# A hybrid decoder layer: sample products in two column halves, and weights, one weight block and the last stage's first chunk queued elsewhere

## The chip, the cores and the metric

The kernel runs on one core of a Trainium2 chip. The metric is the device time of one execution in microseconds (us). Engines are named as in the profile: PE is TensorE (PEld its weight loads), DVE VectorE, ACT ScalarE, POOL GpSimd, SP SyncE, which issues most DMAs. Each engine runs its instructions strictly in the order in which they are queued.

## The reference

One inference step of a one-layer hybrid decoder: eight heads of dilated sliding-window attention beside four heads of an mLSTM matrix memory, with one input and one output projection, for a prompt of 2048 tokens and for 32 sample tokens (8 sequences of 4) that have a cache and a state of their own.

```python
hn = rmsnorm(x, norm_g)
u = hn @ w_in                       # 1024 -> 11 parts
qa, ka, va, za, qb, kb, vb, ob, zb, ib, fb = jnp.split(u, offsets, axis=-1)
# attention: rope on qa, ka; three patterns (window, dilation) = (128,1), (512,4), (2048,16),
# each a partial softmax (m, den, acc); the partials are combined
# mLSTM: qb|kb through a causal convolution of width 4 and SiLU, then in chunks of 128 tokens:
dlog = b[..., :, None] - b[..., None, :] + ic[..., None, :] - m_t[..., :, None]
dmat = jnp.exp(jnp.where(causal, dlog, NEG_INF))
sqk = jnp.einsum('bhtd,bhsd->bhts', qc, kc) * dmat
num = inter[..., None] * jnp.einsum('bhtd,bhde->bhte', qc, C) + jnp.einsum('bhts,bhse->bhte', sqk, vc)
# C, n, m carried to the next chunk; both branches gated by silu(z), then y = x + [att|mlstm] @ w_out
```

## The kernel before

Matrix products run in fp16 with every value split in a high and a low half, so one product of fp32 quality is three matmuls (lines 165, 166 and 167: high·high, high·low, low·high). The program has three stages.

**Projections** (0 to 572 us of the profiled span). Sixteen tiles of 128 prompt tokens meet five blocks of 512 weight columns; `unit(i, j)` is tile i with block j, 24 matmuls of 128x512. Between the units stand: the sample tokens' own projection (`SA.project`, five groups into `ps_dp`, lines 244 and 245), the conversion of six further weight blocks for the mLSTM (`weight_block(j)`, started at the tiles in `BLOCKS`; each ends in `mlstm_part(j)`, which multiplies the sample tokens by that block in two halves, `ps_dm`, lines 316 and 317), and the sample tokens' attention over their caches: a loop over eight sequences (`SA.scores`, lines 359 to 372: a DMA spreads the queries into `d_qb`, POOL multiplies two blocks of keys by them, DVE reduces the three products), then `SA.softmax` (lines 374 to 402, with `ps_den` on PE) and `SA.values`.

**Attention of the prompt** (572 to 893 us). Four pairs of heads, two heads each. `loads(pr)` queues the keys, queries and values of a pair; `head(L, h)` makes scores (`ps_s`), exponentials, transposes (`ps_t`, `th` and `tl`) and products with the values (`ps_o`). Between its steps PE gets other work: the transposes of keys and queries (`ps_k`, `ps_q`), the recurrent state of the sample tokens (class `SampleMLSTM`: `loads`, `prepare`, and `state(b)` for each of eight sequences, whose `dT<-state_C` load POOL copies on line 903) and the first q and k projections of the next stage (`ps_qk`, lines 1161 to 1163, a generator named `early`). After head 0, `prepare` is queued right behind that head's last value product and last POOL step (`issue_after`), and then the SP queue gets three of the mLSTM weight blocks (`wb`, 2 MB each) and the first tokens (`early_x`, 1 MB).

**mLSTM and output** (893 to 1533 us). For each chunk c of 128 tokens: `gate_rows(c)` loads the decay rows `Mb` (POOL adds a mask to them on line 1355, ACT takes four exponentials on line 1359); the convolution turns `ps_qk` into `qk` (ACT, POOL and DVE, lines 1169 to 1190); `gated` makes `ps_st`, `ps_num` and the state; `project_out` multiplies by the output weights `wo`. `loads(c)` fetches the gate `z` and the attention result `A`, which waits until the last attention store to `att_scr` has landed.

The order of each engine's instructions is set when the program is built, by a scheduler that weighs the instructions as the code emits them; `issue_after(x)` forces what follows it behind x on x's engine. The sample products have 64 stationary columns (32 tokens, high and low), so their results take 64 of the 128 partitions of a bank. `sample_sum` adds the high-token and low-token halves: one ACT copy (line 252) and one DVE step (line 256), 32x512 each. The wait for pool tiles is by tag: `dhalf` has one buffer, the banks `proj` have four.

## Time and profile before

| | us |
|---|---|
| median of 3 runs | 1531.36 |
| lowest, highest run | 1527.40, 1534.86 |
| the profiled execution, its own time | 1534.84 |
| its span in the profile | 1533.0 |
| PE busy | 1399.0 (91% of the span) |
| DVE busy | 969.3 (63%) |
| ACT busy | 729.9 (48%) |
| POOL busy | 450.0 (29%) |

The profiled execution took 1.84 us beyond its span and is at the upper end of the three runs. Busy shares are means over three stages that are limited by different things, so the question at each place is what PE waits for there. The profile also gives the granted clock of TensorE, 0.971 on the mean: it is at half in several short stretches, most of which lie about a stall of PE.

### The profile page before, as it was taken

What the parts mean: (1) busy time and instruction counts of PE and PEld (TensorE: products, weight loads), DVE (VectorE), ACT (ScalarE), POOL (GpSimd) and SP (SyncE); (2) the same over time, 40 slices, a digit from 0 to 9 for tenths busy, and PEclk for the clock granted to TensorE, in tenths of its full rate; (3) what the DMA queues carried; (4) which work ended last, traced back from release to release, by engine and by line L of the source; (5) the groups of instructions that cost most, each with busy time, mean ns of one, the idle gap of its engine ahead of it and who ended that gap; (6) DMA issues with size and microseconds to landing.
All of it is one profiled execution on the core that took longest, in us unless ns stands there. A gap on an engine that the chain in (4) does not pass through costs nothing.

```text
span 1533.0 us, 28802 instructions
## 1 busy us (share of the span) xinstructions
PE 1399.0 (91%) x10679; PEld 864.2 (56%) x10679; DVE 969.3 (63%) x2946; ACT 729.9 (48%) x1673; POOL 450.0 (29%) x749
## 2 busy tenths in 40 slices
PE   4899999999989996999898995879999999999996
PEld 2445444444433345878688963556666666666653
DVE  5753765667633246889686813667766666667665
ACT  5365234344344226888677832443444444444433
POOL 1360333443301004645347951211111111111110
PEclk9999999999999998999999997989999999999999
DMA  8354479769779838995948775562555565554312
GB/s 293 123 167 165 139 266 313 271 228 305 281 217 353 286 122 265 350 270 179 239 170 241 264 249 187 188 181 87 176 194 180 165 186 159 173 172 104 77 49 76
DMA packets 153404, 310.95 MB, mean 203 GB/s; under 512 B 13534, under 2 KB 102783, under 8 KB 142687
## 3 DMA queue, kind: packets, MB, share of 16 engines
q1 hardware_dynamic: 149166, 230.10, 48.3%
q0 software_dynamic: 3952, 78.75, 13.9%
q8 instruction: 84, 1.38, 0.4%
q14 instruction: 58, 0.47, 0.1%
q10 hardware_dynamic: 144, 0.26, 0.0%
HBM read 231.80 MB, written 144.38 MB: 245 GB/s over the span
## 4 chain that ended last, share of the span: by engine, by line
PE 32%; DMA 23%; DVE 13%; issue 5%; ACT 4%; POOL 3%; SPq 1%; POOLq 0%; DVEq 0%; ACTq 0%
DMA qi<-g_scr 5%; DMA Mb<-g_scr 5%; PE ps_t L1039 3%; DVE cd L1181 2%; PE ps_out L167 2%; DMA v<-v_scr 2%; DMA kn<-k_scr 2%; PE ps_out L165 2%; PE ps_out L166 2%; PE ps_proj L165 2%; PE ps_proj L167 2%; PE ps_s L1017 2%; PE ps_proj L166 2%; DMA d_kv<-cache_win_v 2%; PE ps_s L1018 2%
## 5 line engine op out<-in xcount | busy, mean ns | idle before, releaser
L165 PE MATMUL ps_proj<-wa,x 128*128 128x512 f16 x640 | 244.9, 385 | 6.8 <-ACT wa L552 4.3
L166 PE MATMUL ps_proj<-wa,x 128*128 128x512 f16 x640 | 245.2, 384 | 2.4 <-POOL wa L111 2.0
L167 PE MATMUL ps_proj<-wa,x 128*128 128x512 f16 x640 | 244.8, 383 | 1.0 <-ACT x L226 1.0
L1026 DVE CUSTOM_DVE_ANT_0 sc<-ps_s,mask,ncqk 128x256 f32<-128x256 f32 (+1 forms) x384 | 142.8, 422 | 26.5 <-PE ps_s L1018 10.4
L1028 POOL TENSOR_SCALAR sc<-sc,o 128x256 f32<-128x256 f32 (+1 forms) x272 | 112.9, 426 | 85.3 <-DVE o L1026 76.7
L1043 DVE SCALAR_TENSOR_TENSOR tl<-ps_t,th 128x512 f16<-128x512 f32 (+1 forms) x152 | 102.6, 681 | 37.8 <-ACT th L1042 37.2
L165 PEld LDWEIGHTS <-x 128*128 128x128 f16 x768 | 73.5, 98 | 93.6 <-issue 22.3
L167 PEld LDWEIGHTS <-x 128*128 128x128 f16 x768 | 73.3, 98 | 85.2 <-issue 11.5
L1181 DVE SCALAR_TENSOR_TENSOR cd<-pre,cw,cd 128x256 f32<-128x256 f32 x168 | 85.9, 516 | 51.5 <-ACT cd L1175 49.6
L166 PEld LDWEIGHTS <-x 128*128 128x128 f16 x768 | 73.1, 98 | 74.4 <-issue 4.9
L367 POOL TENSOR_TENSOR d_kv<-d_kv,d_qb 128x2048 f32<-128x2048 f32 x16 | 72.3, 4538 | 128.3 <-DMA d_qb<-ds_scr 99.6
L1042 ACT ACTIVATE th<-ps_t 128x512 f16<-128x512 f32 (+1 forms) x152 | 90.0, 592 | 37.6 <-PE ps_t L1039 34.8
L167 PE MATMUL ps_out<-wo,yt 128*128 128x512 f16 x256 | 94.9, 379 | 7.8 <-DVE yt L1278 7.0
L1039 PE MATMUL ps_t<-c_id,pr 128*128 128x128 f32 x600 | 100.2, 288 | 1.3 <-DVE tl L1043 1.1
L165 PE MATMUL ps_out<-wo,yt 128*128 128x512 f16 x256 | 97.3, 380 | 2.3 <-ACT yt L1280 1.4
L166 PE MATMUL ps_out<-wo,yt 128*128 128x512 f16 x256 | 97.1, 379 | 0.0
L1355 POOL TENSOR_TENSOR Mb<-Mb,big 128x512 f32<-128x512 f32 x16 | 20.3, 1268 | 249.4 <-DMA Mb<-g_scr 234.5
L1055 PE MATMUL ps_o<-v,th 128*128 128x65 f16 x600 | 80.0, 195 | 14.4 <-ACT th L1042 11.7
L1161 PE MATMUL ps_qk<-cx,wb 128*128 128x256 f16 x256 | 71.0, 277 | 18.3 <-ACT pre L1171 16.5
L1359 ACT ACTIVATE Mb<-Mb,gcols 128x128 f32<-128x128 f32 x64 | 20.5, 390 | 130.5 <-POOL Mb L1355 130.5
L1354 POOL TENSOR_TENSOR qi<-qi,qk 128x128 f32<-128x128 f32 x60 | 29.3, 516 | 171.6 <-DMA qi<-g_scr 162.2
L1056 PE MATMUL ps_o<-v,th 128*128 128x64 f16 x600 | 79.2, 195 | 0.0
(459 smaller groups left out, 3775.1 us busy)
## 6 DMA issues: line engine op xcount, KB each, us to landing
s_win_k<-cache_win_k POOLq DMA_DIRECT2D x32, 1022.0 KB, 8.5
s_win_v<-cache_win_v POOLq DMA_DIRECT2D x32, 1022.0 KB, 7.7
wf<-w_in SPq DMA_DIRECT2D x18, 1024.0 KB
d_kv<-cache_win_k SPq DMA_DIRECT2D x16, 1024.0 KB
d_kv<-cache_win_v SPq DMA_DIRECT2D x16, 1024.0 KB
A<-att_scr SPq DMA_DIRECT2D x16, 792.0 KB
w_scr<-wst SPq DMA_DIRECT2D x12, 1024.0 KB
att_scr<-o SPq DMA_DIRECT2D x9, 1056.0 KB
```

Of the source, the lines that this page charges most:

```text
L165: nc.tensor.matmul(ps, lhsT=xh, rhs=hi[:, kt, cols], start=kt == 0, stop=False)
L166: nc.tensor.matmul(ps, lhsT=xh, rhs=lo[:, kt, cols], start=False, stop=False)
L167: yield nc.tensor.matmul(ps, lhsT=xl, rhs=hi[:, kt, cols], start=False, stop=kt == KT - 1)
L367: nc.gpsimd.tensor_tensor(t, t, qb, ALU.mult)
L1026: nc.vector.tensor_tensor_reduce(sc[:, x:x + n], sp[:, x:x + n], G.mask[:, MASK_END[u[0]] - n:MASK_END[u[0]]], G.ncqk, BIG, ALU.add, ALU.m ...
L1028: pooled = nc.gpsimd.tensor_scalar(sc[:, x:x + n], sc[:, x:x + n], -1.0, nm, ALU.mult, ALU.add)
L1039: nc.tensor.transpose(out=tp[:, c * P:(c + 1) * P], in_=pr[:, c * P:(c + 1) * P], identity=G.idf)
L1042: nc.scalar.activation(th[:, :w], tp[:, :w], AF.Copy, scale=PSC)
L1043: nc.vector.scalar_tensor_tensor(tl[:, :w], tp[:, :w], PSC, th[:, :w], ALU.mult, ALU.subtract)
L1055: nc.tensor.matmul(o, lhsT=th[:, cs], rhs=V[:, 0:65], start=first, stop=False)
L1056: nc.tensor.matmul(o[:, 0:64], lhsT=th[:, cs], rhs=V[:, 66:130], start=False, stop=False)
L1181: eng.scalar_tensor_tensor(d, pre[:, j:j + 256], cw[:, ct, j:j + 1], d, ALU.mult, ALU.add)
```

## The change

It has four parts.

1. `sample_matmuls` and `mlstm_part` no longer add the product with a weight block's high half and that with its low half into the same 64 partitions. A new `sample_pair` puts the first into partitions 0 to 63 and the second into 64 to 127 of the bank. As many matmuls are issued as before. The sum now takes four quarters: ACT copies 64x512 and DVE adds 64x512 (`sample_quarters`), then ACT moves 32x512 and DVE adds 32x512. The output's sample products (`ps_c`) get the same with a tile `dh3`. All in all, ACT and DVE get 12 instructions more each.
2. `BLOCKS` names tile 13 in place of 12 for the fifth weight block. The first half of a block's `ps_dm` stands behind `unit(i, 3)` instead of `unit(i, 2)`, and the second half behind unit 1 of the next tile (`pending`) instead of behind its own tile.
3. `SampleMLSTM.prepare` is put behind all that was queued by then on PE, ACT, DVE and POOL (a new `behind_all`), and the loads of `wb` and `early_x` move behind all SP loads of the second pair of heads.
4. In the last stage `gate_rows(0)` is queued first and the loads of `wo` last, and `gated` of chunk 0 is put behind all that was queued on PE, ACT and DVE.

```diff
--- before
+++ after
-BLOCKS = (5, 7, 9, 11, 12, 14)
+BLOCKS = (5, 7, 9, 11, 13, 14)
...
+@contextmanager
+def behind_all(G, *engines):
+    with ExitStack() as st:
+        for e in engines:
+            st.enter_context(G.tc.issue_after(next(i for i in reversed(G.nc.cur_bb.bb.instructions) if i.engine == e)))
+        yield
...
+def sample_pair(nc, ps, x, hi, lo, first, last):
+    nc.tensor.matmul(ps[0:2 * NS], lhsT=x, rhs=hi, start=first, stop=last)
+    nc.tensor.matmul(ps[2 * NS:], lhsT=x, rhs=lo, start=first, stop=last)
+
 def sample_matmuls(nc, ps, xd, hi, lo, cols):
     for kt in range(KT):
-        x = xd[:, kt].rearrange("p a t -> p (a t)")
-        nc.tensor.matmul(ps, lhsT=x, rhs=hi[:, kt, cols], start=kt == 0, stop=False)
-        nc.tensor.matmul(ps, lhsT=x, rhs=lo[:, kt, cols], start=False, stop=kt == KT - 1)
+        sample_pair(nc, ps, xd[:, kt].rearrange("p a t -> p (a t)"), hi[:, kt, cols], lo[:, kt, cols], kt == 0, kt == KT - 1)
+
+def sample_quarters(nc, t, ps, sc):
+    nc.scalar.activation(t, ps[2 * NS:], AF.Copy, scale=sc[2 * NS:] if sc is not None else 1.0)
+    nc.vector.scalar_tensor_tensor(t, ps[0:2 * NS], sc[0:2 * NS] if sc is not None else 1.0, t, ALU.mult, ALU.add)
 
 def sample_sum(G, pool, out, ps, sc, n, tag="dhalf"):
-    t = pool.tile([P, 512], F32, tag=tag, name="dhalf")[:NS]
-    nc.scalar.activation(t[:, :n], ps[NS:2 * NS, :n], AF.Copy, scale=sc[NS:2 * NS])
-    a, b = ps[0:NS, :n], t[:, :n]
+    t = pool.tile([P, 512], F32, tag=tag, name="dhalf")[:2 * NS, :n]
+    sample_quarters(nc, t, ps[:, :n], sc)
+    a, b = t[0:NS], t[NS:]
...
-    nc.vector.scalar_tensor_tensor(out, a, sc[0:NS], b, ALU.mult, ALU.add)
+    nc.scalar.activation(out, b, AF.Copy)
+    nc.vector.tensor_tensor(out, out, a, ALU.add)
...
             for j in range(5 if i < NT - LATE else 3):
                 pe = unit(i, j)
-                if block is not None and j in (0, 2):
+                if pending is not None and j == 1:
+                    behind(pe, pending)
+                    pending = None
+                if block is not None and j in (0, 3 if i < NT - LATE else 2):
                     behind(pe, block)
...
             gate_unit(i)
-            if block is not None:
-                behind(pe, block)
+            pending = block
...
             L = loads(pr)
+            if pr == 1:
+                with behind_all(G, ENG.SP):
+                    for j in range(3):
+                        nc.sync.dma_start(out=G.wb[j], in_=G.w_scr[j])
+                    nc.sync.dma_start(out=G.early_x.rearrange("p a k t -> p (a k t)"), in_=G.x_scr[0])
             for h in range(2):
...
-                last = head(L, h)
+                head(L, h)
                 if pr == h == 0:
-                    SM.prepare(last)
-                    for j in range(3):
-                        nc.sync.dma_start(out=G.wb[j], in_=G.w_scr[j])
-                    nc.sync.dma_start(out=G.early_x.rearrange("p a k t -> p (a k t)"), in_=G.x_scr[0])
+                    with behind_all(G, ENG.PE, ENG.Activation, ENG.DVE, ENG.Pool):
+                        SM.prepare()
...
+        L = Ctx()
+        gate_rows(0, L)
         xg = [G.early_x, x_load(1)]
         big = one.tile([P, P], F32, tag="big", name="big")
         nc.sync.dma_start(out=big, in_=I["c_causal"])
-        L = loads(0)
-        gate_rows(0, L)
+        loads(0, L)
+        residual(0, L)
         for j in range(2):
             nc.sync.dma_start(out=wo[j], in_=G.w_scr[4 + j])
-        residual(0, L)
...
-            y = gated(c, L, qk, tok, vs[c], ogs[c])
+            with ExitStack() as st:
+                if c == 0:
+                    st.enter_context(behind_all(G, ENG.PE, ENG.Activation, ENG.DVE))
+                y = gated(c, L, qk, tok, vs[c], ogs[c])
```

The tables of the scheduler follow from that. Three places show what the code doesn't tell.

**The SP queue at the first heads.** Before, `wb_5075` to `wb_5077` are the three weight blocks, `qn` and `kn` the queries and keys of the second pair, `v_6680` its first values.

```order
L850 DMA dT<-sg_scr 128x128
L851 DMA dT<-dm_u 32x4x128
L1085 DMA wb_5075<-w_scr 128x8192
L1085 DMA wb_5076<-w_scr 128x8192
L1085 DMA wb_5077<-w_scr 128x8192
L1086 DMA early_x<-x_scr 128x4096
L666 DMA qn<-q_scr 128x16x256
L666 DMA kn<-k_scr 128x6144
L891 DMA dT<-state_C 128x4x128 x2
L865 DMA s_convT<-dT 128x192
L949 DMA v_6680<-v_scr 128x4160
```

After, with `v_6698` the last values of the second pair, and `kn` the keys of the third:

```order
L1125 DMA att_scr<-o_5148 128x16x132
L978 DMA v_6698<-v_scr 8x16x260 x14
L1103 DMA wb_5095<-w_scr 128x8192
L917 DMA s_C<-dT 128x4x128
L1103 DMA wb_5096<-w_scr 128x8192
L1103 DMA wb_5097<-w_scr 128x8192
L1104 DMA early_x<-x_scr 128x4096
L691 DMA kn<-k_scr 128x6144
L937 DMA dm_num<-dT 4x516
L914 DMA dT<-state_C 128x4x128
L917 DMA s_C<-dT 128x4x128
L972 DMA v_8335<-v_scr 128x4160
```

The four large loads stood ahead of the second pair's queries and keys; now they stand ahead of the third pair's keys, and of a `state_C` load.

**The ACT queue at the first head.** `th` and `pr` are steps of the attention; `dT<-dT,scols` (line 879, 902 in the changed kernel) is a step of `prepare`, which waits for POOL's line 876 (899). Before, in the middle of the first head's steps (`o_5130` to `o_5128` are its results):

```order
L1003 ACTIVATE o_5130<-ps_o 128x7x65
L1003 ACTIVATE o_5130<-ps_o 128x2x65
L1042 ACTIVATE th<-ps_t 128x512
L1032 ACTIVATE pr<-sc 128x512
L879 ACTIVATE dT<-dT,scols 32x32 x4
L1042 ACTIVATE th<-ps_t 128x512
L1032 ACTIVATE pr<-sc 128x512
L1042 ACTIVATE th<-ps_t 128x512
```

After, behind the first head's last results and among those of the next:

```order
L1026 ACTIVATE o_5148<-ps_o 128x7x65
L1065 ACTIVATE th<-ps_t 128x512
L1055 ACTIVATE pr<-sc 128x512
L1026 ACTIVATE o_5148<-ps_o 128x2x65
L902 ACTIVATE dT<-dT,scols 32x32 x4
L1065 ACTIVATE th<-ps_t 128x512
L1055 ACTIVATE pr<-sc 128x512
L1065 ACTIVATE th<-ps_t 128x512
```

The step of `prepare` moved from the 254th row to the 308th of ACT, past the rest of head 0.

**ACT and POOL where the last stage begins.** `Mb` of chunk 0 comes first, `Mb` of chunk 1 second; `qk_11736` and `qk_11756` are the last of chunk 0's four convolved pieces. ACT before:

```order
L1185 ACTIVATE qk_11736<-cd 128x256
L1200 ACTIVATE cv<-ps_v,cinv 128x4x128
L1359 ACTIVATE Mb<-Mb,gcols 128x128 x4
L1209 ACTIVATE og<-ps_og,bhinv 128x512 x2
L1359 ACTIVATE Mb<-Mb,gcols 128x128 x4
L1171 ACTIVATE pre<-ps_qk,cinv 128x256
L1169 ACTIVATE tail<-pre 128x3
L1175 ACTIVATE cd<-pre,cw 128x256
L1171 ACTIVATE pre<-ps_qk,cinv 128x256
```

ACT after; the next `Mb` rows, those of chunk 1, stand 25 rows below the first, behind all of chunk 1's `pre` and `qk` rows:

```order
L1384 ACTIVATE Mb<-Mb,gcols 128x128 x4
L1225 ACTIVATE cv<-ps_v,cinv 128x4x128
L1194 ACTIVATE pre<-tail 128x3
L1210 ACTIVATE qk_11756<-cd 128x256
L1225 ACTIVATE cv<-ps_v,cinv 128x4x128
L1234 ACTIVATE og<-ps_og,bhinv 128x512 x2
L1196 ACTIVATE pre<-ps_qk,cinv 128x256
L1194 ACTIVATE tail<-pre 128x3
L1200 ACTIVATE cd<-pre,cw 128x256
```

POOL before (`s_win` are copies of the caches that need no engine's result):

```order
L1184 TENSOR_TENSOR cd<-cd,qk_11736 128x256
L1183 TENSOR_SCALAR qk_11736<-pre,cw 128x256
L1184 TENSOR_TENSOR cd<-cd,qk_11736 128x256
L1189 TENSOR_TENSOR qk_11736<-qk_11736,cd 128x256
L1190 TENSOR_TENSOR qk_11736<-qk_11736,cd 128x256
L1355 TENSOR_TENSOR Mb<-Mb,big 128x512
L264 DMA s_win_k<-cache_win_k 16x16352 x3
L1355 TENSOR_TENSOR Mb<-Mb,big 128x512
L264 DMA s_win_k<-cache_win_k 16x16352
L264 DMA s_win_v<-cache_win_v 16x16352 x2
L1354 TENSOR_TENSOR qi<-qi,qk_11449 128x128
```

POOL after, from chunk 1's `Mb` on:

```order
L1209 TENSOR_TENSOR cd<-cd,qk_11756 128x256
L1380 TENSOR_TENSOR Mb<-Mb,big 128x512
L288 DMA s_win_k<-cache_win_k 16x16352
L288 DMA s_win_v<-cache_win_v 16x16352 x2
L1208 TENSOR_SCALAR qk_11756<-pre,cw 128x256
L1379 TENSOR_TENSOR qi<-qi,qk_11469 128x128
L1379 TENSOR_TENSOR qi<-qi,qk_11510 128x128
L1379 TENSOR_TENSOR qi<-qi,qk_11551 128x128
L1379 TENSOR_TENSOR qi<-qi,qk_11592 128x128
L1209 TENSOR_TENSOR cd<-cd,qk_11756 128x256
L1214 TENSOR_TENSOR qk_11756<-qk_11756,cd 128x256
L1215 TENSOR_TENSOR qk_11756<-qk_11756,cd 128x256
```

On ACT, chunk 1's exponentials no longer stand ahead of the first `pre` of chunk 1. On POOL, chunk 1's `Mb` used to stand behind all of chunk 0's convolution, and now stands ahead of its last four rows. On PE, 48 of chunk 0's 192 `ps_qk` matmuls that stood among the attention's now stand behind it, ahead of `ps_v`.

## Rows read from the trace of the kernel before

**Rows 1.** The page: busy time of each engine, share of the span, instructions.

```profile
PE 1399.0 (91%) x10679; PEld 864.2 (56%) x10679; DVE 969.3 (63%) x2946; ACT 729.9 (48%) x1673; POOL 450.0 (29%) x749
```

**Rows 2.** Windows: stretch, its length, each engine busy (instructions), granted clock, DMA share, GB/s.

```profile
147.00:166.00 19.00, 19.00 (x122) 9.89 (x121) 9.17 (x28) 6.45 (x11) 1.63 (x3) 1.00 0.42 147
355.00:416.00 61.00, 59.51 (x339) 28.31 (x338) 41.24 (x61) 26.33 (x51) 22.71 (x15) 1.00 0.80 274
416.00:436.00 20.00, 15.28 (x75) 7.04 (x74) 8.61 (x23) 10.10 (x25) 2.84 (x6) 0.96 0.81 263
```

**Rows 3.** Tile ps_dp: count, durations in ns (min/median/max), first and last start, forms.

```profile
L244 PE MATMUL ps_dp<-wa,xd x40: 379/379/403, 147.4 to 165.1; 128*64 128x512 f16 x40
...
L252 ACT ACTIVATE dhalf<-ps_dp,wainv x5: 679/679/680, 151.9 to 165.7; 32x512 f32<-32x512 f32 x5
```

**Rows 4.** Groups of PE, 209 to 420 us: count | busy, mean | idle before, its releaser.

```profile
L317 PE MATMUL ps_dm<-wst,xd 128*64 128x512 f16 x32 | 13.8, 430 | 8.6 <-DVE wst L113 8.3
```

**Rows 5.** The same view, 442 to 549 us.

```profile
L418 PE MATMUL ps_dv<-d_kv,d_sc 128*32 128x512 f32 x192 | 24.9, 601 | 1.6 <-DMA d_kv<-cache_win_v 1.6
```

**Rows 6.** Line 367 of the cache loop: starts, its waits, who waited for it.

```profile
L367 POOL TENSOR_TENSOR d_kv<-d_kv,d_qb x16: 4499/4522/4799, 173.3 to 395.4; 128x2048 f32<-128x2048 f32 x16
...
  DMA d_qb<-ds_scr: 99.6, 6
...
  DVE d_sc L372: 45.6, 7
```

**Rows 7.** Chain that ended last, 404 to 437 us: start, length, what.

```profile
414.11 13.18 DMA w_scr<-wst
...
435.85 1.06 PE ps_den L391 x2
```

**Rows 8.** Waits, 590 to 640 us: engine, line, waited for: total, times, longest.

```profile
POOL dT L876 <- DMA dT<-sg_scr: 13.6, 1, 13.6
...
PE ps_o L1055 <- ACT th L1042: 11.7, 1, 11.7
...
PE ps_k L678 <- DMA qn<-q_scr: 2.2, 1, 2.2
```

**Rows 9.** Chain that ended last, 590 to 640 us.

```profile
604.74 32.65 DMA kn<-k_scr
```

**Rows 10.** Windows of the attention.

```profile
595.00:605.00 10.00, 0.29 (x2) 0.13 (x2) 0.41 (x1) 1.88 (x6) 2.00 (x6) 0.50 0.69 160
605.00:609.00 4.00, 3.67 (x37) 3.36 (x38) 3.99 (x15) 2.93 (x8) 1.62 (x4) 0.55 0.96 406
633.00:636.00 3.00, 3.00 (x21) 2.75 (x20) 1.92 (x5) 2.68 (x7) 0.30 (x1) 0.51 1.36 506
675.00:725.00 50.00, 48.51 (x642) 39.62 (x640) 44.26 (x172) 40.53 (x85) 25.89 (x66) 1.00 0.66 220
```

**Rows 11.** Waits, 640 to 893 us.

```profile
POOL dT L903 <- DMA dT<-state_C: 21.5, 4, 10.9
...
PE ps_dn L912 <- POOL dT L903: 7.1, 1, 7.1
```

**Rows 12.** Waits, 893 to 960 us.

```profile
PE ps_qk L1161 <- ACT pre L1171: 16.5, 1, 16.5
```

**Rows 13.** Chain that ended last, 893 to 960 us.

```profile
912.18 21.98 DMA Mb<-g_scr
934.24 1.26 POOL Mb L1355
...
945.70 0.22 PE ps_st L1360 x2
```

**Rows 14.** Windows of the last stage.

```profile
937.00:943.00 6.00, 5.78 (x28) 4.13 (x28) 3.77 (x7) 2.79 (x9) 2.05 (x4) 0.50 1.14 467
1032.00:1066.00 34.00, 34.00 (x232) 21.43 (x230) 24.12 (x80) 12.56 (x36) 5.02 (x6) 1.00 0.37 113
```

**Rows 15.** Tile ps_c, the output product of the samples.

```profile
L244 PE MATMUL ps_c<-wo,dyt x16: 379/379/403, 1066.8 to 1073.9; 128*64 128x512 f16 x16
```

More of the change, by code (lines that the diff above doesn't have):

```diff
@@ L47 @@
 MASK_END = (5 * P, 3 * P, P)
+ENG = mybir.EngineType
 class Ctx:
@@ L290, in project @@
         ps = self.pp.tile([P, 512], F32, tag="proj", name="ps_dp", bufs=4)
-        sample_matmuls(nc, ps[:2 * NS], G.xd, hi, lo, slice(0, 512))
+        sample_matmuls(nc, ps, G.xd, hi, lo, slice(0, 512))
         inv = G.wainv[:, j:j + 1]
@@ L309, in mlstm_part @@
         G, nc = self.G, self.G.nc
-        ps = self.pp.tile([P, 512], F32, tag="proj", name="ps_dm", bufs=4)[:2 * NS]
+        ps = self.pp.tile([P, 512], F32, tag="proj", name="ps_dm", bufs=4)
         def use(half, t):
@@ L314, in use @@
                 kt = half * KT // 2 + i
-                x = G.xd[:, kt].rearrange("p a t -> p (a t)")
-                nc.tensor.matmul(ps, lhsT=x, rhs=t[:, 0, i], start=kt == 0, stop=False)
-                nc.tensor.matmul(ps, lhsT=x, rhs=t[:, 1, i], start=False, stop=kt == KT - 1)
+                sample_pair(nc, ps, G.xd[:, kt].rearrange("p a t -> p (a t)"), t[:, 0, i], t[:, 1, i], kt == 0, kt == KT - 1)
             if half:
@@ L852, in loads, with prepare @@
         nc.gpsimd.memset(self.v[:, :, 128:129], 1.0)
-    def prepare(self, after):
+    def prepare(self):
         G, nc = self.G, self.G.nc
         pre, d, th, tmp, cv, qk, qi, bm, Dm = self.pre, self.d, self.th, self.tmp, self.cv, self.qk, self.qi, self.bm, self.Dm
-        with G.tc.issue_after(after[1].ins):
-            nc.gpsimd.tensor_copy(pre[:, :, :, 0:3], cv)
+        nc.gpsimd.tensor_copy(pre[:, :, :, 0:3], cv)
         ps = self.ps("ps_du")
-        with G.tc.issue_after(after[0].ins):
-            for ct in range(8):
-                nc.tensor.transpose(out=ps[:, ct * NS:(ct + 1) * NS], in_=self.u[:, ct * P:(ct + 1) * P], identity=G.idf[:NS, :NS])
+        for ct in range(8):
+            nc.tensor.transpose(out=ps[:, ct * NS:(ct + 1) * NS], in_=self.u[:, ct * P:(ct + 1) * P], identity=G.idf[:NS, :NS])
         nc.vector.tensor_copy(pre[:, :, :, 3:7], ps[:, 0:8 * NS].rearrange("p (c b t) -> p c b t", c=8, b=NB))
@@ L1056, in head @@
                         nc.tensor.matmul(o[:, 0:64], lhsT=th[:, cs], rhs=V[:, 66:130], start=False, stop=False)
-                        done = nc.tensor.matmul(o, lhsT=tl[:, cs], rhs=V[:, 0:65], start=False, stop=last)
+                        nc.tensor.matmul(o, lhsT=tl[:, cs], rhs=V[:, 0:65], start=False, stop=last)
                         c += 1
@@ L1235, in x_load, with loads @@
             return x16
-        def loads(c):
+        def loads(c, T=None):
             rows = slice(c * P, (c + 1) * P)
-            T = Ctx()
+            T = T or Ctx()
             T.z = pool.tile([P, 2, 512], F32, tag="z", name="z", bufs=2)
```

18 lines of the change are left out of this document (10 added, 8 removed).

## The prediction, made before the changed kernel had run

> **What bounds the kernel now.** I read the busy times first: PE is busy 1399.0 of 1533.0 us [rows 1], so what can be won is matmuls that take less time, or one of PE's waits. Next the windows, to see where PE is not full, and the waits there, to see who was last. In the projections PE is nearly full, 59.5 of 61 us in 355 to 416 [rows 2], apart from waits ahead of `ps_dm` [rows 4] and a thin stretch from 416 to 436. In the attention the first head has a hole: 0.29 us of PE in 595 to 605 [rows 10], for a DMA that POOL waits for, and PE behind it [rows 8]. Later PE is full there, 48.5 of 50 us, with DVE at 44.3 and ACT at 40.5 close behind [rows 10]. Where the last stage begins there is a second hole, 16.5 us [rows 12]. After that PE is full, 34.00 of 34 us [rows 14]. The sum is made against the profiled execution, 1534.84 us (span 1533.0 and 1.84 around it); that stands 3.5 us above the median of 1531.36.
>
> **Column halves, projections.** In `ps_dp` the first matmuls of the 40 pairs start from 147.4 to 165.1 us [rows 3], so a pair takes 0.454 us, one matmul 0.227, and all 18.2. Do the two halves run at once? `ps_dv`, which uses quarters of the columns, is the nearest row: 192 matmuls of 601 ns in only 24.9 us [rows 5], so four to five are under way at a time. I take it that halves overlap as well: 18.2 becomes 9.1; at the other end nothing is won. The 32 pairs of `ps_dm` [rows 4] take 14.5 us at the same pace, of which half, 7.3, can go, and so can the 8.6 us that PE idles ahead of them [rows 4], since a block's products now stand a unit or more later. Were PE alone the limit, the projections would win 9.1 + 7.3 + 8.6 = 25 us.
>
> PE is not alone. The cache loop needs nothing from it: 16 multiplications of 4.5 us start from 173.3 to 395.4 us, POOL waits 99.6 us for `d_qb`, and DVE waits 45.6 us for POOL [rows 6]. DVE, which empties PE's banks, is queued in the order of that loop, so PE can't run far ahead of it; at the end PE waits for the loop's softmax at `ps_den`, 435.85 [rows 7]. So I count what the loop's chain wins: about 2 us by an earlier start (the sample rows come out of `project` sooner, but their sum has grown, below), and from the softmax, which stood 13.2 us behind the store of block 12's halves [rows 7]. That block is now at tile 13, behind the softmax; I take 8 of the 13. PE then has 18 matmuls of 0.227, 4 us, more to do behind `ps_den`. Net: 2 + 8 − 4 = 6 us won; ends 0 and 25.
>
> **The longer sum.** Each group of sample products now takes ACT 64x512, DVE 64x512, ACT 32x512, DVE 32x512, where one copy of 32x512 took 0.679 us [rows 3]. If the number of partitions costs nothing (an assumption), a group takes some 1.4 us more, with one `dhalf` buffer: five groups in `project`, four in `mlstm_part`, one of gates, two of the output. With four banks PE isn't held by that, and in 147 to 166 us DVE is busy 9.17 and ACT 6.45 of 19 [rows 2], which hides it. If that cover is gone, five times 1.4, 7 us, go into the loop's start. I count nothing beyond the 2 us above; ends 0 and −7.
>
> A group's 16 matmuls take 3.6 us and would take 1.8, while each step of its sum stays near 0.7 [rows 3]. The Trainium skill, "TensorEngine Tiling (Array Packing)", Performance Considerations, warns that tiling speeds up TensorE but not the emptying of PSUM, which may become the bottleneck. By it the five groups would follow each other at the sum's pace, four times 0.679 or 2.7 us, 13.6 in place of 9.1, and the time would be 4 us longer than I say. Its Tile-to-Partition Mapping adds that column tiling disables Fast Weight Load; no run shows yet what that does to these loads.
>
> **First head.** POOL waited 13.6 us for `dT`, and PE 11.7 us in the end [rows 8]; the waiting steps of `prepare` now stand behind head 0. The DMA won't land later, since only what follows it on its queue moves, and head 0's rest fills the time. So the 11.7 us go, and with them half clock: the granted clock is 0.50 in 595 to 605 and 0.55 in 605 to 609 with PE busy 3.67 us [rows 10], some 2 us. The next stall, 2.2 us for `qn` [rows 8], had its load, and `kn`'s of 32.65 us [rows 9], behind 7 MB of weights; these loads now go ahead of the weights. It too left half clock, 0.51 in 633 to 636 with PE busy 3.00 [rows 10], 1.5 us. The place holds 17 us.
>
> What is late next: the weights now stand ahead of the third pair's `kn` and of a `state_C` load. 7.3 MB at 406 GB/s [rows 10] are 18 us of DMA, issued at some 655 to 675 us; in 675 to 725 the DMAs are free a third of the time, 17 us [rows 10]. The order has also moved the third pair's key transposes and the state's copies down, so the two about meet. `state_C` loads already cost POOL 21.5 us in four waits and PE 7.1 in one [rows 11]; I take 5 us for another such wait, ends 0 (it just fits) and 18 (the whole transfer is waited for). Net: 12 us won; ends −1 and 17.
>
> **Start of the last stage.** Chunk 1's `Mb` lands 21.98 us after its issue, POOL takes it at 934.24 [rows 13], ACT's exponentials stand ahead of `pre`, and PE gets its banks back after 16.5 us [rows 12], at clock 0.50 until 943 with 5.78 us busy [rows 14], 3 us more. In the new order `pre` doesn't wait for it, so that stall goes. What is late next is POOL: the same `Mb` now stands ahead of the last rows of chunk 0's convolution, which `ps_st` needs. Chunk 0's `Mb`, as large, no longer goes just ahead of it; I estimate that it lands a third of its 22 us sooner, at 927. POOL has then 1.26 us for the mask [rows 13] and eleven shorter rows of some 0.6: 8 us, so 935. PE has, from the end of the attention at 893, 96 matmuls of 512 columns at 0.227 us and 48 + 96 `ps_qk` of 256 at half of that, 38 us, and comes there at 931. A new wait of 4 us; chunk 0's last `ps_st`, at 945.70 before [rows 13], comes at some 935, 11 us sooner. The 48 `ps_qk` are 5.4 us that the attention no longer has to do; with DVE at 88% there [rows 10] I give back 3. Net: 14 us; ends 4 (the `Mb` lands when it did) and 19 (no new wait).
>
> **Output of the samples.** 16 pairs of `ps_c` from 1066.8 to 1073.9 us [rows 15] take 7.6, on a PE without gaps [rows 14]: half, 3.8, less some for the longer sum, 3; ends 0 and 3.8.
>
> **Sum.** 6 + 12 + 14 + 3 = 35: 1534.84 − 35 = 1499.8. By the median it would be 1496.4. I forecast 1498, between the two. The ends of all terms together are −4 and 65 us.
>
> **The rivals.**
> PE alone is the limit of the projections: 25 us in place of 6, 1479. For it: PE is 98% full [rows 2]. Against: it already waits for the loop's end.
> The column halves don't run at once: the projections still win some 4 us by the loop, the output nothing: 1503. For it: no row shows halves of fp16. Against: the quarters [rows 5].
> The change doesn't do what it says at the last stage: chunk 1's `Mb` lands as late as before, and the wait comes back ahead of `ps_st`; 14 becomes 4, 1508. For it: `A`, ahead of it, must still wait for the attention's last store. Against: `pre`, and DVE behind it, go on meanwhile.
> The late weights collide, the one that ends on the other side. The third pair's `kn` and a `state_C` load stand behind 7.3 MB, as the second pair's `kn` did for 32.65 us [rows 9]. If PE waits for the whole 18 us, runs at half clock for 3 more, and each of four later states waits 10.9 us, as the longest did [rows 11], the price is 65 us, against 40 won elsewhere and here: 1558. It decides from a price of 40 us on. Against: the states' copies moved down. A price near 20, more likely, gives 1513.
>
> **How the numbers follow.** Forecast 0.5 (1487 to 1508), PE alone 0.1, halves 0.13, moved wait 0.12, collision 0.15 (0.1 near 20 us, 0.05 beyond 40). The range 1482 to 1522 leaves out PE alone and the full collision. A measurement of this kernel tells about 0.5%, 7.7 us, from no change. Faster by more, below 1523.7: 0.85. Within: 0.09. Slower: 0.06.
>
> **What would show it.** Right: pairs of `ps_dp` and `ps_c` some 0.23 us apart; no wait ahead of `ps_dm`; `ps_den` some ten us sooner with PE waiting for it; PE full from 590 to 620; no wait of 16 us for `pre`, but one of some 4 ahead of chunk 0's `ps_st`. Wrong: pairs still 0.45 us apart; POOL waiting over 11 us for `state_C`, or PE for `kn`, at the third pair; projections shorter by over 15 us.

## The result, and the profile after

The change made the kernel slower: 1550.6 us (median of four runs, 1544.45 to 1554.0) against 1533.11 of the kernel before on the same chip. The ratio is 1.0112, with a 95% interval of 1.0079 to 1.0145, so some 17 us were lost where 35 were forecast as won. The profiled execution took 1549.89 us, its span 1548.1. PE does the work with 13 us less of busy time than in [rows 1], and idles more; the page of after:

```profile
PE 1385.7 (90%) x10679; PEld 857.7 (55%) x10679; DVE 972.5 (63%) x2958; ACT 739.2 (48%) x1685; POOL 449.0 (29%) x749
```

Three times cut the span into parts: the start of the first score (`ps_s`), of the last value product of the attention (`ps_o`), and of the last output product (`ps_out`).

| us | before | after | difference | forecast |
|---|---|---|---|---|
| start to first score | 572.7 | 561.5 | −11.2 | −6 |
| attention (first score to last `ps_o`) | 320.3 | 320.1 | −0.2 | −12 |
| last `ps_o` to last `ps_out` | 630.3 | 656.8 | +26.5 | −17 |

Each column is one profile. Seven kernels (after and, of the experiments below, e1, e3, e4, e6, e7 and e9) have the same order of instructions on PE, DVE, ACT and POOL up to the first score; in their profiles it starts at 554.6 to 570.7 us, 562 on the mean. So the −11.2 holds to some 8 us.

**The column halves run at once.** The tiles `ps_dp` and `ps_c` of after (count, durations in ns, first and last start, forms):

```profile
L255 PE MATMUL ps_dp<-wa,xd x40: 379/379/403, 147.3 to 156.6; 128*64 128x512 f16 x40
L256 PE MATMUL ps_dp<-wa,xd x40: 379/379/403, 147.4 to 156.8; 128*64 128x512 f16 x40
...
L255 PE MATMUL ps_c<-wo,dyt x16: 379/379/403, 1078.1 to 1082.0; 128*64 128x512 f16 x16
```

40 pairs take 9.5 us in place of 18.2 [rows 3], 16 pairs of `ps_c` 3.9 in place of 7.1 [rows 15]: a pair starts every 0.24 to 0.26 us, where one matmul started every 0.23 before. The weight loads of these matmuls take 110 ns before and after.

**Projections.** The waits of PE from 166 to 436 us in after (line, waited for: total, times, longest). Nothing waits ahead of `ps_dm` [rows 4] any more, but PE now waits for its banks:

```profile
PE ps_proj L177 <- DVE t L536: 11.2, 3, 4.8
PE ps_xt L237 <- DVE dhalf L268: 5.3, 1, 5.3
```

POOL's reduction for the softmax, one row of the tile `d_mx`, comes 14.1 us sooner; before, then after:

```profile
L382 POOL PARTITION_ALL_REDUCE d_mx<-d_mx x1: 1082/1082/1082, 417.9 to 417.9; - x1
```

```profile
L404 POOL PARTITION_ALL_REDUCE d_mx<-d_mx x1: 1085/1085/1085, 403.8 to 403.8; - x1
```

**First head.** The waits from 570 to 640 us, and pieces of the chain there (start, length, what):

```profile
PE ps_k L703 <- DMA qn<-q_scr: 15.0, 1, 15.0
...
POOL dT L877 <- DMA dT<-dm_u: 13.8, 1, 13.8
```

```profile
581.88 7.91 DMA v<-v_scr
589.81 0.64 SPq L876
590.56 0.32 SPq L691
590.91 6.20 DMA qn<-q_scr
597.16 1.03 PE ps_k L703 x8
```

The hole of [rows 8] is still there. PE now comes to the second pair's query transposes at 582 us, where before it came there at 629: 76 score matmuls stand ahead of them in its order, before 160. Their load is issued only at 590.91, since SP first queues the first pair's values one behind the other. POOL waits 13.8 us as before, now on line 877, a memset in `SampleMLSTM.loads`, which the change did not move. Before, the same memset (line 852) stood one row behind the row of `prepare` that POOL waited for, and its own load landed 0.8 us later; in the waits of [rows 8] it is

```profile
POOL dT L852 <- DMA dT<-dm_u: 0.4, 1, 0.4
```

It runs 30.7 us behind the first score before, 31.0 after. The first pair of heads, from its first score to the second pair's, takes 74.5 us in both; the second pair takes 77.8 us before and 83.7 after, the third and fourth are 3.5 and 2.6 us shorter.

**Third pair.** The waits from 690 to 780 us. PE waits for the keys queued behind the late weights, POOL for states, as long as before [rows 11]:

```profile
POOL dT L926 <- DMA dT<-state_C: 22.3, 4, 9.7
...
PE ps_k L703 <- DMA kn<-k_scr: 14.3, 2, 10.8
```

In 675 to 725 us PE is busy 38.96 of 50 us at a granted clock of 0.86 (columns as in [rows 10], where it was 48.51 at 1.00, though after is some 11 us further on in its work):

```profile
675.00:725.00 50.00, 38.96 (x521) 33.51 (x520) 33.92 (x140) 32.67 (x66) 19.69 (x52) 0.86 0.78 297
```

**Start of the last stage.** The waits from 881 to 990 us, and the chain there:

```profile
POOL Mb L1380 <- DMA Mb<-g_scr: 47.1, 2, 35.7
ACT Mb L1384 <- POOL Mb L1380: 26.9, 2, 17.4
...
PE ps_v L177 <- ACT cv L1225: 13.2, 1, 13.2
...
PE ps_qk L1186 <- ACT pre L1196: 5.2, 1, 5.2
...
PE ps_v L177 <- ACT pre L1196: 3.9, 1, 3.9
```

```profile
895.08 20.67 DMA Mb<-g_scr
915.82 1.27 POOL Mb L1380
...
917.41 0.97 ACT Mb L1384 x3
918.38 0.58 ACT cv L1225
919.01 0.58 PE ps_v L177
...
950.33 1.18 ACT Mb L1384 x4
951.53 0.70 DVE W L1389
```

The stall of [rows 12] has become three. The longest, 13.2 us, ends when ACT empties a bank (`cv`), and ACT had stood 17.4 us at the exponentials of an `Mb` that POOL could not mask before it landed. By the buffer numbers of the program this `Mb` is chunk 1's, and the trace agrees: POOL had masked one `Mb`, the first queued, at 893 us already. Chunk 0's exponentials come only at 950 us, and the step that uses them, `W`, right behind. Of the two groups of `Mb` rows that "The change" finds on ACT, 25 rows apart, the upper is thus chunk 1's and the lower chunk 0's. The first `ps_out` starts 108.1 us behind the last `ps_o`, before 83.6.

### The profile page after: what moved, and what is told of

Its sections match the earlier page's. It is cut to its first block, busy times and chain, and to the rows that moved or that the text cites. A ratio compares the mean times of both kernels' runs of the same rounds, so it can differ in the third digit from the quotient of the medians.

```text
span 1548.1 us, 28812 instructions
## 1 busy us (share of the span) xinstructions
PE 1385.7 (90%) x10679; PEld 857.7 (55%) x10679; DVE 972.5 (63%) x2958; ACT 739.2 (48%) x1685; POOL 449.0 (29%) x749
## 3 DMA queue, kind: packets, MB, share of 16 engines
q0 software_dynamic: 3952, 78.75, 13.8%
## 4 chain that ended last, share of the span: by engine, by line
PE 37%; DMA 26%; DVE 17%; issue 6%; POOL 6%; ACT 6%; SPq 2%; POOLq 0%; DVEq 0%; ACTq 0%
DMA Mb<-g_scr 5%; DMA qi<-g_scr 4%; PE ps_proj L179 3%; PE ps_proj L177 3%; PE ps_proj L178 3%; DMA d_qb<-ds_scr 3%; PE ps_t L1062 3%; DMA kn<-k_scr 3%; DMA v<-v_scr 2%; POOL d_kv L389 2%; PE ps_out L179 2%; DVE cd L1206 2%; PE ps_out L177 2%; PE ps_out L178 2%; PE ps_s L1040 1%
## 5 line engine op out<-in xcount | busy, mean ns | idle before, releaser
L177 PE MATMUL ps_proj<-wa,x 128*128 128x512 f16 x640 | 245.2, 385 | 17.8 <-DVE t L536 11.2
L177 PEld LDWEIGHTS <-x 128*128 128x128 f16 x768 | 73.5, 98 | 97.9 <-issue 13.8
L1186 PE MATMUL ps_qk<-early_x,wb 128*128 128x256 f16 x256 | 71.6, 280 | 10.5 <-ACT pre L1196 9.5
```

The source lines that it names most:

```text
L177: nc.tensor.matmul(ps, lhsT=xh, rhs=hi[:, kt, cols], start=kt == 0, stop=False)
```

## Experiments

Ratios are to the kernel before on the same chip, with 95% intervals. That kernel took 1539 to 1544 us on these chips, some 10 more than in the trace of before, so stages are compared among the experiments. "Rest" is from the last `ps_o` to the last `ps_out`, in us of one profile; "late" counts those of chunk 0's 192 `ps_qk` matmuls that stand behind the attention's last score in PE's order (before 24, after 72; of these, 48 of after also stand behind the attention's last value product, and none of before).

| | ratio | interval | attention | rest | late |
|---|---|---|---|---|---|
| e1 parts 1 and 2 | 0.9921 | 0.9896–0.9945 | 319.6 | 637.7 | 24 |
| e2 parts 1, 2, 4 | 0.9917 | 0.9890–0.9944 | 321.0 | 638.6 | 24 |
| e3 parts 1, 2, 3 | 1.0017 | 0.9987–1.0046 | 326.1 | 649.6 | 72 |
| e4 after, weights early | 0.9899 | 0.9837–0.9962 | 323.7 | 630.7 | 4 |
| e5 e4, memset early | 0.9936 | 0.9909–0.9963 | 332.9 | 631.1 | 4 |
| e6 after, weights behind keys | 1.0009 | 0.9985–1.0033 | 321.2 | 649.3 | 24 |
| e7 after, exponentials in order | 0.9970 | 0.9948–0.9992 | 317.7 | 638.2 | 72 |
| e8 e5, exponentials in order | 0.9923 | 0.9894–0.9951 | 328.9 | 625.0 | 4 |
| e9 after, keys held | 1.0116 | 1.0081–1.0151 | 322.3 | 666.4 | 72 |
| e10 e8, keys held | 0.9893 | 0.9866–0.9919 | 324.6 | 630.5 | 24 |
| e11 e10, weights behind keys | 0.9867 | 0.9812–0.9921 | 312.8 | 622.6 | 4 |
| e12 part 1 | 1.0000 | 0.9969–1.0030 | 324.7 | 635.9 | 24 |
| e13 part 2 | 1.0019 | 0.9998–1.0040 | 320.6 | 635.1 | 24 |
| e14 e11 without part 1 | 0.9957 | 0.9935–0.9979 | 322.2 | 621.4 | 4 |

### Which part loses: e1, e2, e3

e1 is the kernel before with parts 1 and 2; e2 adds part 4, e3 part 3. From after, e1 and e2 take out

```diff
-                if pr == 1:
-                    with behind_all(G, ENG.SP):
-                        ... wb and early_x
...
-                    with behind_all(G, ENG.PE, ENG.Activation, ENG.DVE, ENG.Pool):
-                        SM.prepare()
+                    SM.prepare(last)
+                    ... wb and early_x
```

and e1 and e3

```diff
-                if c == 0:
-                    st.enter_context(behind_all(G, ENG.PE, ENG.Activation, ENG.DVE))
```

with the order of the last stage's first loads.

> The kernel before with parts 1 and 2 alone (column halves, later weight block). In the trace of the changed kernel the first scores of the attention start 11.2 us sooner than before, and the samples' output product takes 3.4 us less. If these two parts are independent of the rest, as both theories hold, this kernel is 12 to 15 us faster than before: 1518 to 1521 us. If the gain of the projections came from the other parts, or is given back at the waits of the attention, within 3 us of before.

> Parts 1, 2 and 4, without 3 (prepare and the weight loads as before). Theory F (part 4 makes the loss: chunk 0's exponentials are forced behind chunk 1's, which wait for a DMA): the 26 us that the changed kernel loses where the last stage begins are lost here too, 1540 to 1547. Rival W (part 3's late weights make it: the first q and k projections and their convolution are pushed behind the attention): the start of the last stage is as before, with its 16 us wait for pre, and the kernel is as fast as parts 1 and 2 alone, 1517 to 1521.

> Parts 1, 2 and 3, without 4. Theory F: the last stage starts without the 13 us wait for the banks of ps_v, and the kernel is near 1520. Rival W: 48 q and k projections and the convolution on POOL still stand behind the attention, POOL and ACT still make PE wait 15 to 25 us there, and the kernel is at 1540 to 1550.

Parts 1 and 2 win 0.8%, 12 us. Part 4 on them wins and loses nothing (0.9917). Part 3 costs 0.96%, 15 us (0.9921 to 1.0017), and in the profiles the rest is 12 us longer, the attention 6.5. By e2 and e3 theory F fails and rival W, the weights' place, holds. The waits of PE from 881 to 966 us in e1, e2 and e3:

```profile
PE ps_qk L1186 <- ACT pre L1196: 16.4, 1, 16.4
```

```profile
PE ps_qk L1186 <- ACT pre L1196: 11.9, 1, 11.9
PE ps_yt L1301 <- ACT yh L1340: 7.0, 1, 7.0
```

```profile
PE ps_qk L1186 <- ACT og L1234: 13.7, 2, 12.3
PE ps_qk L1186 <- ACT pre L1196: 5.2, 1, 5.2
PE ps_v L177 <- ACT pre L1196: 2.4, 1, 2.4
```

In e1 the stall is that of [rows 12], to 0.1 us. In e2 it is 4.5 us shorter, and 7.0 come back 40 us later: `pre` still waits there for ACT, which stands 14.7 us at chunk 1's exponentials. In e3 more is lost, ahead of work that the attention used to hide: 72 of chunk 0's `ps_qk` matmuls, which need `wb` and `early_x`, now stand behind its last score, 24 in e1 and e2. At the third pair e3 also waits 9.7 us for `kn`, e1 and e2 not at all.

### The weights' place alone: e4 and e6

e4 is after with the weights at their old place, so part 3 is reduced to `prepare`; e6 is after with the weights behind the second pair's queries and keys, ahead of its values. The edit of e6:

```diff
                 pair_loads(G, pr)
+                if pr == 1:
+                    with behind_all(G, ENG.SP):
+                        for j in range(3):
+                            nc.sync.dma_start(out=G.wb[j], in_=G.w_scr[j])
+                        ... early_x
```

> Parts 1, 2, 4 and the half of 3 that puts prepare behind head 0; the weight loads stay right behind head 0. Theory F: 1530 to 1540, since the start of the last stage is lost as in the changed kernel. Rival W: 1503 to 1512: 12 to 15 us from parts 1 and 2, some 10 from the first head's wait of 11.7 us, and no loss behind.

> The changed kernel, with the three weight blocks and early_x queued on SP behind the second pair's keys and queries, but ahead of its values. In this order 24 of chunk 0's q and k projections are left behind the attention (72 in the changed kernel, 24 before), and the third pair's kn no longer stands behind the weights. Theory W (the place of the weight loads behind the values makes the loss): the 10.8 us wait for kn at 702 and the 9 us of waits for pre behind the attention go, the 15 us wait for qn stays: 0.985 to 0.995. Rival F (part 4 makes the loss): 1.000 or more.

With all else as in after, early weights give 0.9899 in place of 1.0112: 33 us for the order of four DMAs. e4 leaves 4 matmuls, after 72. e6 takes the wait for `kn` at the third pair away and leaves 24, but still measures 1.0009, where theory W had put it at 0.985 to 0.995, with 12.9 us for `qn` at the first head and 8.7, 5.8 and 7.0 at the start of the last stage. Its rest is 11 us longer than e2's, which also leaves 24 and has the same forced order. All of it falls ahead of the first `ps_out`, where PE idles 6.8 us longer than in e2 and is busy 4.0 longer with as many matmuls; where these waits come from no run separates. So the number of late matmuls is not all that the weights' place costs.

In e4 `prepare` stands behind head 0, and the first head still has its hole; waits from 580 to 645 us, and the load of the next pair's queries in the chain:

```profile
POOL dT L877 <- DMA dT<-dm_u: 13.5, 1, 13.5
...
PE ps_o L1078 <- ACT th L1065: 12.3, 1, 12.3
```

```profile
587.61 27.51 DMA qn<-q_scr
```

### The first head's wait: e5, e9, e10

e5 is e4 with the memset of one column ahead of the DMA that fills the others.

```diff
+        nc.gpsimd.memset(self.v[:, :, 128:129], 1.0)
         nc.sync.dma_start(out=self.v[:, :, 0:128], ...)
-        nc.gpsimd.memset(self.v[:, :, 128:129], 1.0)
```

> As e4 (parts 1, 2, 4, prepare behind head 0, weights early), but POOL's memset of the column beside a loaded tile, in SampleMLSTM.loads, is queued ahead of that tile's DMA instead of behind it. In e4 PE still waited 12.3 us at 590, and POOL 13.5 us in that memset for the DMA. Theory M (the memset is what holds the first head): the 12 us wait goes, and with it half clock: 10 to 14 us below e4, ratio 0.980 to 0.984 against before. Rival S (the serial loads of the values on SP hold the head's next products too): PE waits there for v or qn instead, at most 3 us gained, 0.988 to 0.990.

POOL's wait goes and head 0 ends earlier: the second head's scores begin at 592.6 us (598.4 in e4). Then PE waits for the next pair's queries, whose load now stands right behind the weights; waits from 580 to 645 us and chain:

```profile
PE ps_k L703 <- DMA qn<-q_scr: 16.1, 1, 16.1
```

```profile
596.89 27.92 DMA qn<-q_scr
```

The 12.3 us came back as 16.1, and the first pair takes 80.0 us (e4 72.3). This is a load that nobody had waited for long while PE was late. e9 and e10 hold the second pair's transposes further back, near where they stood before the change (behind 168 score matmuls; before 160, after 76), e9 in after, e10 in e8 (below):

```diff
+            if L.pr == 1 and h == 0:
+                with G.tc.issue_after(G.mark.ins):
+                    stacks(G, h, st, ...)
...
```

where `G.mark` is a score matmul of the 13th batch of the second head.

> The changed kernel with one edit: the transposes of pair 1's queries and keys for its first head are held behind the 13th score batch of head (0,1), so they stand at ps_s index 168 in TensorE's queue, where the changed kernel has them at 76. Nothing else is told to move. Theory 'only the place': the 15.0 us of idle TensorE at 597 us (ps_k behind the DMA of qn) were a wait for a load that lands near 612 us; at index 168 TensorE comes to it near 625 us, so the wait is gone, no other takes its place beyond the 10 us of the memset, and the first head ends some 5 to 12 us sooner; ratio to before 1.000 to 1.007 (the changed kernel 1.0112). Rival 'the wait is the load's chain': the memset still holds GpSimd near 590 us until dT lands, TensorE waits there in its place (10 us or more, as in the experiment on parts 1 and 2), and the time stays at 1.010 to 1.013. The late weights' other waits (kn at the third pair, the start of the last stage) stay in both.

> The kernel of e8 (parts 1 and 2, prepare behind head 0, weights at their old place, the memset ahead of its DMA, the last stage's first gate rows first, the exponentials of chunk 1 in the order of GpSimd) with pair 1's transposes held behind the 13th score batch of head (0,1). In e8 TensorE waited 15.9 us at 622 us for qn, whose load was queued right behind the 7.3 MB of weights. Theory 'the 7.3 MB must pass': qn lands near 638 us whatever stands ahead on TensorE; the transposes are due at index 168, near 620 us, so TensorE still waits 5 to 16 us: ratio to before 0.989 to 0.993, as e8 (0.9923). Rival 'only the place': the wait is gone and the ratio is 0.983 to 0.986.

e9 measures 1.0116, as after: the wait for `qn` is gone, and the memset's stands in its place. (The expectation has the load landing at 612 us; 597 is right, the wait ends there.) In e10 the 7.3 MB must pass: 13.4 us for `qn`, as the first theory said (the load lands at 620 us, not near 638). The waits of PE from 580 to 645 us in e9 and e10:

```profile
PE ps_o L1083 <- ACT th L1070: 10.1, 1, 10.1
```

```profile
PE ps_k L703 <- DMA qn<-q_scr: 13.4, 1, 13.4
```

So three things end within some 30 us of each other there: the sample rows for POOL, the next pair's queries, and the weights ahead of them. Mending one shows the next.

### The start of the last stage: e7 and e8

e7 is after without the forced order of chunk 0, and with chunk 1's and 2's exponentials held behind the ACT work of the chunk ahead of them:

```diff
+                    if c in (1, 2):
+                        st.enter_context(tc.issue_after(state["exps"]))
                     e = nc.scalar.activation(Mb[:, h], Mb[:, h], AF.Exp, ...)
...
-                if c == 0:
-                    st.enter_context(behind_all(G, ENG.PE, ENG.Activation, ENG.DVE))
```

e8 has this, early weights, the early memset and `prepare` behind head 0.

> The changed kernel without behind_all on chunk 0, and with ACT's exponentials of chunk 1 held behind chunk 1's convolution and those of chunk 2 behind chunk 1's; gate_rows(0) first, weights late as in the changed kernel. Theory F (ACT's early exponentials of chunk 1 cost the 13.2 us wait for the banks of ps_v): that wait goes, and the kernel gains 12 to 18 us on the changed one, 0.994 to 1.000. Rival P (POOL, which waits for the same Mb ahead of chunk 0's last convolution, is the limit anyway): PE waits as long ahead of ps_st, at most 5 us gained, 1.006 to 1.011.

> Parts 1 and 2, prepare behind head 0, weights early, the memset ahead of its DMA, gate_rows(0) first, no behind_all on chunk 0, and ACT's exponentials of chunk 1 held behind chunk 1's convolution. If the three mechanisms are what I take them for (memset 12 us, Mb ahead of pre 16 us, parts 1 and 2 12 us), they add up to 35 to 40 us: 0.973 to 0.977. If chunk 1's Mb only moves the wait to ps_st, 0.980 to 0.985.

e7 wins 1.4% over after (0.997): 22 us for the order of some ACT instructions. Its first `ps_out` comes 84.8 us behind the attention, after's 108.1. Of the 13.2 us for `cv` 0.8 are left; the waits for `pre` stay; e7 too has 72 late matmuls. PE from 875 to 985 us in e7:

```profile
PE ps_qk L1186 <- ACT pre L1196: 5.2, 1, 5.2
PE ps_v L177 <- ACT pre L1196: 4.3, 1, 4.3
...
PE ps_v L177 <- ACT cv L1225: 0.8, 1, 0.8
```

e8's rest, 625.0 us, is 13 below e1's, but it loses 15.9 us to `qn` in the first head and ends at e1's ratio, 0.9923, where 0.973 to 0.977 was expected.

### A version that beats both: e11

> As e10, but the weights are queued on SyncE behind the loads of pair 1's queries and keys and ahead of its values (as in e6), not ahead of all three. Theory (weights and keys no longer in each other's way): qn lands near 605 to 615 us, TensorE comes to the transposes near 620, no wait there and none over 4 us for kn at the third pair; only 4 of chunk 0's 192 ps_qk matmuls are left behind the attention, so the start of the last stage is as in e8 (first ps_out 70 to 76 us behind the last ps_o): 12 to 16 us less than e8, ratio to before 0.982 to 0.986. Rival 'the wait is carried on': pair 1's values now land behind the 7.3 MB, and TensorE waits 8 to 16 us for v at ps_o near 640 to 650 us; ratio 0.989 to 0.994.

e11 is e10 with the weights where e6 has them. It took 1520.94 us (1509.99 to 1529.99) against 1539.45 before: 0.9867. The execution profiled is the fastest, 1509.99. The waits of PE from 580 to 645 us, then from 875 to 985:

```profile
PE ps_t L1072 <- ACT pr L1065: 7.3, 1, 7.3
PE ps_o L1088 <- DMA dT<-dm_u: 1.8, 1, 1.8
```

```profile
PE ps_yt L1306 <- ACT yh L1345: 7.8, 2, 4.8
PE ps_qk L1191 <- ACT pre L1201: 5.0, 1, 5.0
```

The queries are in time, and no wait for values took their place; the attention is the shortest of all, 312.8 us. The first pair takes 58.9 us, where it took 74.5 before and in after, and 72 to 80 in all other runs but e14 (58.7). But the second pair takes 89.7 us (before 77.8, e10 82.7): the 7.3 us stand there, behind a state load that POOL waits for, 10.6 us. In e14, with the same three changes, it takes 96.5, and the attention is 322.2 again. So half of the gain or more is carried on to the next wait once more. That e11 beats e10 or e4 its four runs don't settle: the intervals overlap.

### Parts 1 and 2 apart: e12, e13, e14

e12 is the kernel before with part 1, e13 with part 2, e14 is e11 without part 1.

```text
 e12:  BLOCKS = (5, 7, 9, 11, 12, 14), blocks used where they were; sample_pair
 e13:  BLOCKS = (5, 7, 9, 11, 13, 14), pending; one column group
```

> The kernel before with the sample products in the two halves of the columns and their longer sum, and nothing else: the weight blocks stay at tiles 5, 7, 9, 11, 12, 14 and are used where they were. Parts 1 and 2 together were 0.9921, some 12 us, of which 3.4 are the output. Theory 'halves': TensorE's time is what the projections lacked, so the halves alone bring the first score from 572.7 to 562 to 565 us and the ratio is 0.992 to 0.994. Rival 'the block's place': the cache loop's end sets the pace, as forecast; the halves alone bring 2 us there (the loop's earlier start), the rest came with block 12 at tile 13 and the later use of the blocks; first score at 568 to 572 us, ratio 0.995 to 0.998, and TensorE waits ahead of ps_dm and ps_am as in the kernel before (3 to 4 us each).

> The kernel before with part 2 alone: the weight blocks at tiles 5, 7, 9, 11, 13, 14, each used one unit of work or more later; the sample products stay in one column group (128x64), as before. Parts 1 and 2 together measured 0.9921, part 1 alone 1.000 (0.9969 to 1.003). Theory 'the place is worth it all': the 8.3 us of TensorE ahead of ps_dm and the 3.0 ahead of ps_am go, the softmax no longer stands 13 us behind block 12's store; ratio 0.992 to 0.994, ps_den near 422 us. Theory 'only together': TensorE, 98% full there, must first have time to come to the moved work; the ratio is 0.997 to 1.000, and the two parts' gains do not add up.

> The best kernel so far (e11: 0.9867, interval 0.9812 to 0.9921) with its sample products back in one column group and the shorter sum, all else the same. Theory 'the halves are worth 8 us once the blocks' place has changed': ratio 0.991 to 0.993, first score 8 us later than in e11, the output 3 to 4 us longer (pairs of ps_c 0.45 us apart). Rival 'the halves bring the output's 3 us at most': ratio 0.987 to 0.989.

Alone, neither wins anything (1.0000 and 1.0019). Together they win 12 us, and in the mended kernel the halves are worth 0.9%, 14 us (0.9957 against 0.9867, intervals apart, by four runs of e11 on another chip). None of the three fell where it was expected, and the size of the last is rough: the second pair's 89.7 and 96.5 us, where the halves do nothing, are in it. PE's waits from 166 to 445 us in e12, e13 and e1, and where each has the softmax's `ps_den`, from the tile `d_mx`:

```profile
PE ps_dm L256 <- DVE wst L125: 14.3, 5, 6.6
```

```profile
PE ps_proj L177 <- DVE t L526: 10.2, 3, 4.3
PE ps_dv L430 <- ACT wst L146: 4.2, 1, 4.2
```

```profile
PE ps_proj L177 <- DVE t L536: 12.0, 4, 5.1
```

```profile
L413 PE MATMUL ps_den<-d_mx,ones x2: 634/634/634, 434.8 to 435.3; 128*32 128x256 f32 x2
```

```profile
L403 PE MATMUL ps_den<-d_mx,ones x2: 379/391/403, 434.2 to 434.5; 128*32 128x256 f32 x2
```

```profile
L413 PE MATMUL ps_den<-d_mx,ones x2: 379/391/403, 420.1 to 420.4; 128*32 128x256 f32 x2
```

With the halves alone PE comes sooner to `ps_dm` and waits there for the converted weights, 14.3 us in place of 8.3. With the later place alone that wait is 1.6, but PE has no time to win from it: it is busy all 20 us of 416 to 436. In both the softmax ends where it did, at 434 to 436 us; only together does it end at 420. All runs bear that out: `ps_den` stands at 415 to 423 us in after and e1 to e11, and at 434 in e14, which lacks the halves.

## Why the prediction was wrong

**Column halves: right.** I took that 18.2 us become 9.1; it was 9.5. With four banks the longer sum did not set the pace of the matmuls. It did set its own: ACT begins the five groups' first copies from 150.3 to 163.2 us, 3.2 us apart, where a group's matmuls take 1.9. The Trainium skill, "TensorEngine Tiling (Array Packing)", Performance Considerations, says that after a speedup of four the copies out of PSUM may become the bottleneck. At a speedup of two the trace agrees for what waits for the sums, and not for PE, whose matmuls took 9.5 us and not the 13.6 that I had worked out for that case. The 5.3 us at `ps_xt` are not the sum's length: the gates' sum stood behind a DVE step of 32x512 that took 4.71 us, where one of this shape took 0.40 before it (last section).

**Projections: the right place, by other terms.** 11.2 us in place of 6, in one profile; e1's ratio, 12 us with some 3 of the output, says 9. The loop's softmax does come sooner: `ps_den` stands at 421.1 against 435.85 [rows 7], 14.7 sooner, where I took 2 + 8. But the 2 for an earlier start aren't there: the first multiplication starts at 173.4 us, before 173.3, and the third group's sum, the last of the queries, keys and values, ends at 160.2, before 160.3. And the 8 for the softmax don't lie where I had put them, in the store of block 12: from POOL's reduction to `ps_den`, in which most of that store ran, it takes 17.3 us, before 18.0. What won lies ahead: the loop's last multiplication starts at 388.0 in place of 395.4, 7.4 sooner, and the way from there to the reduction is 6.7 shorter. What shortened these two no run separates. What I did not see either is that the two parts need each other (e12, e13). The rival of PE alone (25) falls by e12: PE's saved time turned into waits.

**The longer sum: hidden from PE, as forecast.** DVE is busy 13.3 of 19 us in 147 to 166, ACT 9.8, and PE stays full there. The assumption that the number of partitions costs nothing holds: ACT's copy of 64x512 took 0.683 us. That the sum leaves the loop 2 us sooner does not.

**First head: wrong, 0 in place of 17.** The failing step is "So the 11.7 us go": the first pair takes 74.5 us as before. I had put POOL's wait on `prepare` alone. The next row on the same queue, the memset beside the DMA-filled columns, waits for a load of the same batch (13.8 us in after, 13.5 in e4, 11.3 in e9), and behind it stands `qn`, whose load is not early while SP queues values one by one (after) or weights (e5, e10). "The DMA won't land later" was true, to 0.3 us, and beside the point: another row waited for it, and PE had come earlier to the next load.

**Late weights: the price in the attention was foreseen, and its place elsewhere was not.** The wait for `kn` at the third pair (10.8 us, forecast as some 5, ends 0 and 18), with a granted clock of 0.86 about it, is the collision rival's, and it is between the forecast and that rival's likelier price of 20. The larger price fell in the last stage, which no rival named, and this is the step that failed: there I let the late weights cost nothing but PE's time. They feed chunk 0's `ps_qk`, 72 of which were left behind the last score. I had counted 48 more as 5.4 us of PE's work, without the banks that ACT and the convolution must empty for them (`pre`, `og`: 5.2, 2.4 and 13.7 us in e3). How the weights' place makes the rest of its price is open (e6).

**Start of the last stage: wrong, +26.5 in place of −14 and −3.** The failing step is "In the new order `pre` doesn't wait for it, so that stall goes". `pre` still stands behind that `Mb`, and ACT's copy `cv` now does too, so PE stops for `cv` (13.2 us) before it comes to `pre`. In e2, which has part 4 without the late weights, it waits 11.9 us for `pre` itself. I took ACT's first `Mb` instructions for chunk 0's. They are chunk 1's: `behind_all` held only chunk 0's back, and the scheduler moved chunk 1's ahead, in front of ACT's copies out of PE's banks. The estimate of when an `Mb` lands (927) was even too late: 915.8. Part 4 cost 15 us where the weights are late (e3 to after) and nothing where they are early (e2), although chunk 1's exponentials stand ahead there too; taking the forced order out and putting the exponentials in order won 22 (e7). Which of these two won how much was not tried apart; e3, which leaves out part 4 whole and so also has the loads in the old order, is at 1.0017, 15 of the 22 below after.

**Output: right.** `ps_c` takes 3.9 us in place of 7.1, 3.2 won where I took 3. In the rest of the stage it can't be told apart from other differences.

## What to carry to other kernels

Before you count a wait as won, follow the queue of the waiting engine and the queue of its load for the next 30 us, and name the next load that engine will come to; here three in a row were due within some 30 us. Mending one (e5) or two (e8, e10) moved the wait; with all three mended the first pair took 15.6 us less (e11, e14), but the second took 7 us more than in e10 in e11, and 14 more in e14. A DMA's place in a queue also decides when its consumers may be scheduled: moving weights by one pair of heads moved 48 matmuls (72 in place of 24) out of an attention that hid them. Where a forced order holds one chunk back, read with buffer numbers which chunk comes forward in its place.

## What the runs showed of the hardware

Two column groups of 64 with fp16 inputs run at once: a pair every 0.24 us where one matmul started every 0.23, matmuls of 379 ns each as before. The load of a pair's queries behind 7.3 MB on the same queue took 27.9 us from issue to landing (e5), one not behind them 6.2 (after).

VectorE and GpSimd can hold each other up. The DVE step ahead of the gates' sum (line 328, 32x512) and POOL's first multiplication come at nearly the same time. Where DVE's step starts with POOL's or just ahead, it takes 0.41 us and POOL's 4.79 and 4.75 (e1, e3; other multiplications take 4.5). Where it starts 0.09 and 0.05 us behind POOL's, it takes 4.71 and 4.73 and ends 0.3 us behind POOL's end (after, e7). PE then waits 5.3 and 5.5 us at `ps_xt`; in e1 and e3 it waits 0.7 and 0.4. The order of the instructions is the same in all four, so it is luck, less than 0.1 us, which of the two comes first.

And the projections vary: e3 and e7 have the same order of instructions up to the first score, and it starts at 554.6 us in one profile and at 570.7 in the other, on two chips; the wait just told is 5 of these 16 us. A stage's time in one profile is no measure of a few us there; the ratios are.
